# A state space layer's decay matrices from absolute values, without a mask product, with its first scan begun later and two parts of its output split ahead

## The chip, the cores and the metric

The kernel runs as one program on one core of a Trainium2 chip. Five engines of that core work beside each other, each on its own queue of instructions: TensorE (PE, matrix products; its weight loads are listed as PEld), VectorE (DVE), ScalarE (ACT), GpSimd (POOL) and SyncE (SP, which issues most DMAs). The metric is the time of one execution in microseconds on the device. Three runs of the kernel before took 2714.09, 2718.22 and 2720.84; the median is 2718.22.

## The reference, cut to what matters

The program is a chain of eight layers over 512 tokens of width 1024, all in fp32. The layer in question is the second, a Mamba-2 mixer: a projection in, a convolution of four taps with a Silu, 8 groups of 4 heads of width 64 with a state of 128, a scan over 4 chunks of 128 tokens, a gated norm and a projection out.

```python
def step(state, inp):                       # one chunk of 128 tokens
    xc, dtc, bc, cc = inp
    acs = jnp.cumsum(dtc * a, axis=1)
    seg = acs[:, :, None] - acs[:, None, :]
    decay = jnp.exp(jnp.where(mask, seg, -jnp.inf))       # mask: lower triangle
    cb = jnp.einsum("blgn,bsgn->blsg", cc, bc)
    xdt = xc * dtc[..., None]
    y_diag = jnp.einsum("blsg,blsgr,bsgrp->blgrp", cb, decay, xdt)
    y_off = jnp.einsum("blgn,bgrpn->blgrp", cc, state) * jnp.exp(acs)[..., None]
    decay_to_end = jnp.exp(acs[:, -1:] - acs)
    new_state = (state * jnp.exp(acs[:, -1])[..., None, None]
                 + jnp.einsum("bsgn,bsgr,bsgrp->bgrpn", bc, decay_to_end, xdt))
    return new_state, y_diag + y_off
...
y = y + d_skip.astype(jnp.float32).reshape(SSM_GROUPS, SSM_HPG)[:, :, None] * xs
g = (y.reshape(b, s, D_INNER) * jax.nn.silu(z.astype(jnp.float32))).reshape(b, s, SSM_GROUPS, NORM_GROUP)
g = g * lax.rsqrt(jnp.mean(g * g, axis=-1, keepdims=True) + EPS)
g = g.reshape(b, s, D_INNER) * norm_w.astype(jnp.float32)
return g.astype(h.dtype) @ w_out
```

dt is positive and a is negative, so acs falls along a chunk: in the lower triangle seg is never positive, and above it it is never negative.

## The kernel before, in words

**Products.** A product of fp32 operands is made of three matmuls in fp32r (`mm3`, L179 to L181): high part by high part, and the two mixed ones. Weights come by DMA in pieces of 1 MB (`raw`); ACT casts a piece to its high part (wh, L166) and DVE subtracts (wl, L167), for 128x1024 at a time. Activations are split in the same way (xh and xl, ghi and glo, yh and yl, ow). PSUM is used through two pools of four banks each, `psum` (tag ps) and `pacc`; a tile of `psum` is free again when its last reader is done.

**Order.** PE's order in the stage is the order of the code (`manual_schedule(engines={PE})`). The order on the other engines is worked out by a scheduler when the kernel is built, from its own costs for the whole program, so an edit in one stage can shift instructions of ACT and DVE in another.

**The state space stage** runs from about 379 to 853 us. `ssm_groups` goes through 8 groups. For a group, `group` makes four products of 8 steps (`product`, ps_in: B, C and two halves of x, each followed by `conv_silu`) and four z chunks (ps_z, 8 short products each; group 0's z comes with dt ahead of it). It yields 12 times, after each half of a product and each z chunk, and 8 times for group 0. At each yield the scan of the group before is moved one step on (`next(scan, None)`), so a scan's small matmuls lie between products of the next group, which cover its waits.

**A scan** (`ssm_scan`): the first one begins with `ssm_decay`, which makes from dta (dt times a) the sums of a chunk: acsT (the sums on partitions, in two parts), nacs (minus the sums), eacs, etot and edte (exponentials of the sums, of the whole, and of the rest times dt; `dtg` is dt in the scan's order). Then come two pairs of heads: L498 spreads a head's sums over 128 partitions (ps_R, a selecting matrix by acsT), L499 adds a constant `late` in bf16, a large negative number above the diagonal, and ACT takes Exp with the bias nacs for each of the 4 chunks (L503): the decay matrix G. The steps after: transposes of x (ps_x, L511; copies xs L512 on ACT), of B (ps_b, L516), and C by B (ps_cb, L521); on POOL xde = xs by edte (L523) and, after xdt, xs by d_skip (L529); on DVE xdt (L525) and, four times, G by ps_cb (L527). Two steps later, for each chunk, G by xdt into ps_y (L541), the state's products (L543, L546), the sum y, z's gate and a square sum. Last the norm's scale on DVE, the transposes ps_g (L575, two tiles of `psum`) and the copies gt by the norm's weight (L577, ACT).

**The output projection** (`row_steps`) is a generator as well: a step `next(out)` is two products of a 128 wide column with one of the 16 gts, split to high and low by `part`. The last scan has no group left beside it; the steps of `out` lie between its steps, 16 up to its end, and they use parts 0 to 7, which take over the tiles (`xw`) of the layer's input. Parts 8 to 15 follow.

**Other stages that the prediction speaks of.** In the hybrid stage (the seventh, about 2220 to 2440 us) POOL gates pieces of its output weights (L1151), ACT and DVE split them (ow, L172 and L173), and the last of its attention units run meanwhile: scores, Exp to pr (L1310), transposes and copies pT (L1318, by ACT for odd heads), values, and yc, which PE transposes (L1141) before the output products ps_out. In the routed stage (the last) DVE reduces a count to `most` and casts it to an integer, most_i (L1639), which the engines read into a register.

Of the kernel before, what the change touches and what calls it, by code (L numbers as in the profile page):

```python
# [7 lines left out]
F32 = mybir.dt.float32  # L8
# [5 lines left out]
AF = mybir.ActivationFunctionType  # L14
# [4 lines left out]
P = 128  # L19
S = 512  # L20
NT = S // P
# [8 lines left out]
SG, SN, SH = 8, 128, 32  # L30
# [3 lines left out]
def blk(i, n=P):  # L34
    return slice(i * n, (i + 1) * n)
# [42 lines left out]
class Stream:  # L78
# [38 lines left out]
    def next(self, width, eng=None, pieces=1):  # L117
        raw = self.load(width)
        wh = self.pool.tile([P, max(width, 1024)], F32R, tag="wh", name="wh")
        wl = self.pool.tile([P, max(width, 1024)], F32R, tag="wl", name="wl")  # L120
        for i in range(pieces):
            c = blk(i, width // pieces)
            self.K.split(wh[:, c], wl[:, c], raw[:, c], eng)
        return wh, wl


class Kern:
# [220 lines left out]
    def ssm(self, x, wcols, st, V, R):  # L348

        nc, C = self.nc, self.consts  # L350
        with ExitStack() as ctx:
            ctx.enter_context(self.tc.manual_schedule(engines={PE}))
            gtp = self.pool(ctx, "sgt", 16)
            gts, hs = [], []
            out = self.row_steps(16, hs, st, lambda d, p: nc.vector.tensor_add(x[d], x[d], p))

            def part(pool, b, hi, lo):
                hh = pool.tile([P, S], F32R, tag=hi, name="ghi")
                hl = pool.tile([P, S], F32R, tag=lo, name="glo")
                self.split(hh, hl, gts[b])  # L360
                hs.append((hh, hl))

            with ExitStack() as c2:
                scan = self.ssm_groups(c2, gtp, gts, x, wcols, st, V, R)
                xpart = lambda b: part(self.xw, b, f"xh{b}", f"xl{b}")
                next(scan)
                xpart(0)
                xpart(1)
                for i, _ in enumerate(scan):
                    if i < 6:  # L370
                        xpart(i + 2)
                    for _ in range(1 + (i > 5)):
                        next(out)
            hp = self.pool(ctx, "shp", 8)
            for b in range(8, 16):
                part(hp, b, "hh", "hl")
            for _ in out:
                pass

    def ssm_groups(self, ctx, gtp, gts, x, wcols, st, V, R):  # L380

        nc, C = self.nc, self.consts
        t1 = self.pool(ctx, "st1", 1)
        t2 = self.pool(ctx, "st2", 2)
# [7 lines left out]
        E = dict(xw=xw, V=V, R=R)  # L392
# [42 lines left out]

        scan = iter(())
        for g in range(SG):
            for _ in group(g):
                next(scan, None)
            for _ in scan:  # L440
                pass
            scan = self.ssm_scan(g, t1, t2, gtp, gts, E if g == 0 else dict(E))
        for _ in scan:
            yield

# [38 lines left out]
        nc.scalar.activation(E["edte"], perm(pz[:, :W]), AF.Exp)  # L484
        nc.vector.tensor_mul(E["edte"], E["edte"], E["dtg"])

    def ssm_scan(self, g, t1, t2, gtp, gts, E):

        nc, C, V, R = self.nc, self.consts, E["V"], E["R"]
        if g == 0:  # L490
            self.ssm_decay(t1, E)
        bT, cT, xT, zs = E["bT"], E["cT"], (E["xT0"], E["xT1"]), E["zs"]
        bc = lambda t: t[:, g].rearrange("p c h -> p (c h)").unsqueeze(2).to_broadcast([P, 16, 64])
        G = []
        for h in range(4):
            hd = 4 * g + h
            pR = self.psum("ps_R")
            nc.tensor.matmul(pR, C["sel"][:2 * SH, hd:hd + 1].to_broadcast([2 * SH, P]), E["acsT"], start=True, stop=False)  # L498
            nc.tensor.matmul(pR.rearrange("p (a b) -> p a b", b=P), C["identb"],  # L499
                             C["late"].unsqueeze(1).to_broadcast([P, NT, P]), start=False, stop=True)  # L500
            G.append(t1.tile([P, NT, P], F32, tag=f"G{h}", name=f"G{h}"))
            for c in range(NT):
                nc.scalar.activation(G[h][:, c], pR[:, blk(c)], AF.Exp, bias=E["nacs"][:, g, c, h:h + 1])  # L503
            if h % 2:
                yield
        xs = t1.tile([P, 16, 64], F32, tag="xs", name="xs")
# [12 lines left out]
        pc = self.psum("ps_cb")  # L519
# [3 lines left out]
        nc.gpsimd.tensor_mul(xde, xs[:, :12], bc(E["edte"])[:, :12])  # L523
        xdt = t1.tile([P, 16, 64], F32, tag="xdt", name="xdt")
        nc.vector.tensor_mul(xdt, xs, bc(E["dtg"]))  # L525
        for h in range(4):
            nc.vector.tensor_mul(G[h], G[h], pc.rearrange("p (a b) -> p a b", b=P))  # L527
        dsk = R["d_skip"][:, blk(g, 4)].unsqueeze(1).to_broadcast([P, NT, 4])
        nc.gpsimd.tensor_mul(xs.rearrange("p (c h) k -> p c h k", c=NT), xs.rearrange("p (c h) k -> p c h k", c=NT),  # L529
                             dsk.unsqueeze(3).to_broadcast([P, NT, 4, 64]))  # L530
# [7 lines left out]
        for c in range(NT):  # L538
# [5 lines left out]
            if c < NT - 1:  # L544
                pst = self.psum("ps_st")
                nc.tensor.matmul(pst[:, :256], bt[:, c], xde[:, 4 * c:4 * c + 4].rearrange("p a b -> p (a b)"),  # L546
                                 start=True, stop=True)
# [1592 lines left out]
```

## Time and profile before

| | |
|---|---|
| median of three runs | 2718.22 us |
| the profiled execution | 2712.77 us |
| its span | 2710.9 us |
| PE busy | 2601.5 us, 96% |
| DVE busy | 1546.7 us, 57% |
| ACT busy | 1073.6 us, 40% |
| POOL busy | 240.7 us, 9% |

PE is the engine that sets the time; DVE and ACT have room over the span as a whole. A share of the whole span says little of one stage, though, so the rows below are of short stretches. A row of the timeline gives the start and the length in us, the engine, the line and the operation, its tiles (out<-in), the shape, a count, and in brackets the idle time of that engine just before and the instruction that ended it. Matmuls overlap by a part of their length: a product of 512 columns is listed at 0.39 us and the next one begins 0.23 later at the full clock of 2.4 GHz; at 1.2 GHz it is 0.63 and 0.43. A row of the windows gives for each engine its busy time and count in the stretch, PEld between PE and DVE, then the granted clock of PE as a share of full speed, and what the DMAs did.

### The profile page before, as it was taken

To read this page: it belongs to the slowest core of one execution; us is meant where nothing else is said; L and a number is where in the kernel's file an instruction comes from. 1 tells how busy PE (TensorE), PEld (TensorE's weight loads), DVE (VectorE), ACT (ScalarE), POOL (GpSimd) and SP (SyncE) were. 2 spreads that over 40 slices of the span, in tenths; PEclk is the share of its full clock that TensorE was granted. 3 is DMA by queue.
4 is the path that set the end of the run, shared out by engine and by line. 5 is a ranking of instruction groups with operands and counts; after the bars stand their busy time and mean duration, and the time that the engine had idled before them with its cause. 6 is when DMAs were issued, how large, how long until landed. Compare 5 with 4: busy or idle time off the path is not lost. (4 is left out here: it accounts for less than half of the span.)

```text
span 2710.9 us, 32248 instructions
## 1 busy us (share of the span) xinstructions
PE 2601.5 (96%) x12798; PEld 2142.6 (79%) x12798; DVE 1546.7 (57%) x2548; ACT 1073.6 (40%) x1805; POOL 240.7 (9%) x180
## 2 busy tenths in 40 slices
PE   8999999999999999999999999999999989997993
PEld 6888887888878888888888897888888877766782
DVE  5334357676765454656534368655434365567986
ACT  4222245546443222233212245643213234444882
POOL 0000001111100000000000003100000001223324
PEclk9999998999999999999999999999999999898996
DMA  4222221212143243534423221012223222034893
GB/s 153 98 99 99 93 96 47 78 63 78 63 164 132 93 156 118 179 108 160 160 86 109 93 86 61 17 49 94 96 90 109 93 74 88 14 124 168 305 332 114
DMA packets 56472, 300.77 MB, mean 111 GB/s; under 512 B 12002, under 2 KB 12514, under 8 KB 27130
## 3 DMA queue, kind: packets, MB, share of 16 engines
q1 hardware_dynamic: 50096, 285.41, 29.9%
q0 software_dynamic: 4176, 7.39, 0.7%
q10 hardware_dynamic: 2042, 5.84, 0.6%
q8 instruction: 102, 1.67, 0.3%
q14 instruction: 56, 0.46, 0.1%
HBM read 290.68 MB, written 15.75 MB: 113 GB/s over the span
## 5 line engine op out<-in xcount | busy, mean ns | idle before, releaser
L166 ACT CAST wh<-raw 128x1024 fp32r<-128x1024 f32 (+3 forms) x494 | 485.7, 994 | 1100.9 <-PE ps_p L180 378.6
L167 DVE TENSOR_TENSOR wl<-raw,wh 128x1024 fp32r<-128x1024 f32 (+3 forms) x494 | 576.0, 1176 | 385.6 <-ACT wh L166 375.9
L179 PE MATMUL ps_p<-xh,wh 128*128 128x512 f32 x1408 | 550.1, 391 | 6.7 <-ACT xh L172 6.7
L180 PE MATMUL ps_p<-xl,wh 128*128 128x512 f32 x1408 | 549.7, 390 | 0.0
L181 PE MATMUL ps_p<-xh,wl 128*128 128x512 f32 x1408 | 549.5, 390 | 0.0
L179 PEld LDWEIGHTS ps_p<-xh,wh 128*128 128x128 f32 x1408 | 265.4, 188 | 62.4 <-ACT xh L172 6.7
L180 PEld LDWEIGHTS ps_p<-xl,wh 128*128 128x128 f32 x1408 | 265.3, 188 | 56.1 <-DVE xl L173 1.0
L181 PEld LDWEIGHTS ps_p<-xh,wl 128*128 128x128 f32 x1408 | 265.2, 188 | 55.5
L179 PE MATMUL ps_d<-hh,wh 128*128 128x512 f32 x704 | 279.1, 396 | 0.0
L181 PE MATMUL ps_d<-hh,wl 128*128 128x512 f32 x704 | 279.1, 396 | 0.0
L180 PE MATMUL ps_d<-hl,wh 128*128 128x512 f32 x704 | 279.1, 396 | 0.0
L294 DVE TENSOR_TENSOR h<-ps_p,g 128x512 f32<-128x512 f32 x88 | 60.8, 691 | 229.4 <-PE ps_p L181 229.0
L291 DVE TENSOR_TENSOR g<-ps_p,rb 128x512 f32<-128x512 f32 x88 | 60.3, 689 | 177.5 <-PE ps_p L181 177.5
L181 PEld LDWEIGHTS ps_d<-hh,wl 128*128 128x128 f32 x704 | 132.6, 188 | 32.3
L180 PEld LDWEIGHTS ps_d<-hl,wh 128*128 128x128 f32 x704 | 132.6, 188 | 32.3
L179 PEld LDWEIGHTS ps_d<-hh,wh 128*128 128x128 f32 x704 | 132.6, 188 | 32.2
L179 PE MATMUL ps_in<-xh,wh 128*128 128x512 f32 x336 | 140.9, 419 | 0.7 <-ACT wh L166 0.7
L181 PE MATMUL ps_in<-xh,wl 128*128 128x512 f32 x336 | 132.5, 394 | 0.5 <-DVE wl L167 0.5
L180 PE MATMUL ps_in<-xl,wh 128*128 128x512 f32 x336 | 132.1, 393 | 0.0
L181 PEld LDWEIGHTS ps_in<-xh,wl 128*128 128x128 f32 x336 | 63.6, 189 | 15.1 <-DVE wl L167 1.0
L674 POOL TENSOR_TENSOR kro<-prj,kg 128x64 f32<-128x64 f32 x1 | 0.4, 367 | 844.5 <-ACT prj L732 844.5
L961 DVE SCALAR_TENSOR_TENSOR macc<-mraw,c_act,macc 128x1024 f32<-128x1024 f32 x42 | 53.9, 1284 | 37.0 <-DMA mraw<-w_mod 36.7
(577 smaller groups left out, 4224.1 us busy)
## 6 DMA issues: line engine op xcount, KB each, us to landing
raw<-w_ffn SPq DMA_DIRECT2D x131, 1024.0 KB, 4.9
raw<-w_moe SPq DMA_DIRECT2D x48, 1024.0 KB, 7.5
raw<-w_ssm SPq DMA_DIRECT2D x31, 1024.0 KB, 5.1
mraw<-w_mod SPq DMA_DIRECT2D x48, 512.0 KB, 4.4
raw<-w_hyb SPq DMA_DIRECT2D x9, 1024.0 KB, 4.7
expert_out<-zero SPq DMA_DIRECT2D x8, 512.0 KB, 9.9
raw<-w_mla SPq DMA_DIRECT2D x4, 1024.0 KB
yback<-expert_out SPq DMA_DIRECT2D x8, 512.0 KB, 4.6
```

The lines of the kernel that those rows point to most:

```text
L166: a = self.nc.scalar.copy(hi, src)
L167: b = (eng or self.nc.vector).tensor_sub(lo, src, hi.bitcast(F32))
L179: mm(out, ah, bh, start=start, stop=False)
L180: mm(out, ah, bl, start=False, stop=False)
L181: mm(out, al, bh, start=False, stop=stop)
L291: nc.vector.tensor_mul(g, pg, r)
L294: nc.vector.tensor_mul(h, pu, g)
L674: nc.gpsimd.tensor_mul(w, x2, b)
L961: nc.vector.scalar_tensor_tensor(acc, w, ca[:, k:k + 1], acc, op0=ALU.mult, op1=ALU.add)
```

## The change

- `late` and `identb` are no longer multiplied in. ACT takes for each head and chunk the absolute value of the sum's difference (Abs with the bias nacs), and one Exp of 128x512 with scale -1 follows for the head. In the lower triangle that is the same decay; above it it is a value between 0 and 1 in place of 0.
- The mask is put on C by B: `cb` is ps_cb times the triangle, one DVE operation of 128x512 for a group, and G is multiplied by cb, from SBUF, instead of by ps_cb.
- The first scan has a step more, after `ssm_decay`, and in group 1 the steps are given by (0, 0, 1, 2, 2, 1): it begins two steps later, and two later yields take two steps.
- Parts 0 and 1 have tiles of their own (`sgp`), so they are split as soon as their gts are there; `first` is called when scan 5 has been created. In the last scan a step of `out` follows each step from the first on, and two from the ninth on, so that it is 16 at its end as before. The first pair of heads, then an output step, then the second pair now follow ps_g; before, both pairs came first.

```diff
--- before.py
+++ after.py
@@ -361,15 +361,12 @@
                 hs.append((hh, hl))
 
             with ExitStack() as c2:
-                scan = self.ssm_groups(c2, gtp, gts, x, wcols, st, V, R)
-                xpart = lambda b: part(self.xw, b, f"xh{b}", f"xl{b}")
-                next(scan)
-                xpart(0)
-                xpart(1)
+                sp = self.pool(ctx, "sgp", 2, side="right")
+                scan = self.ssm_groups(c2, gtp, gts, x, wcols, st, V, R, lambda: [part(sp, b, "fh", "fl") for b in range(2)])
                 for i, _ in enumerate(scan):
                     if i < 6:
-                        xpart(i + 2)
-                    for _ in range(1 + (i > 5)):
+                        part(self.xw, i + 2, f"xh{i}", f"xl{i}")
+                    for _ in range(1 + (i > 7)):
                         next(out)
             hp = self.pool(ctx, "shp", 8)
             for b in range(8, 16):
@@ -377,7 +374,7 @@
             for _ in out:
                 pass
 
-    def ssm_groups(self, ctx, gtp, gts, x, wcols, st, V, R):
+    def ssm_groups(self, ctx, gtp, gts, x, wcols, st, V, R, first):
 
         nc, C = self.nc, self.consts
         t1 = self.pool(ctx, "st1", 1)
@@ -435,11 +432,14 @@
 
         scan = iter(())
         for g in range(SG):
-            for _ in group(g):
-                next(scan, None)
+            for i, _ in enumerate(group(g)):
+                for _ in range((0, 0, 1, 2, 2, 1)[i] if g == 1 and i < 6 else 1):
+                    next(scan, None)
             for _ in scan:
                 pass
-            scan = self.ssm_scan(g, t1, t2, gtp, gts, E if g == 0 else dict(E))
+            scan = self.ssm_scan(g, t1, t2, gtp, gts, dict(E), None if g else E)
+            if g == 5:
+                first()
         for _ in scan:
             yield
 
@@ -484,23 +484,24 @@
         nc.scalar.activation(E["edte"], perm(pz[:, :W]), AF.Exp)
         nc.vector.tensor_mul(E["edte"], E["edte"], E["dtg"])
 
-    def ssm_scan(self, g, t1, t2, gtp, gts, E):
+    def ssm_scan(self, g, t1, t2, gtp, gts, E, live=None):
 
         nc, C, V, R = self.nc, self.consts, E["V"], E["R"]
-        if g == 0:
-            self.ssm_decay(t1, E)
+        if live is not None:
+            self.ssm_decay(t1, live)
+            E = dict(live, **E)
+            yield
         bT, cT, xT, zs = E["bT"], E["cT"], (E["xT0"], E["xT1"]), E["zs"]
         bc = lambda t: t[:, g].rearrange("p c h -> p (c h)").unsqueeze(2).to_broadcast([P, 16, 64])
         G = []
         for h in range(4):
             hd = 4 * g + h
             pR = self.psum("ps_R")
-            nc.tensor.matmul(pR, C["sel"][:2 * SH, hd:hd + 1].to_broadcast([2 * SH, P]), E["acsT"], start=True, stop=False)
-            nc.tensor.matmul(pR.rearrange("p (a b) -> p a b", b=P), C["identb"],
-                             C["late"].unsqueeze(1).to_broadcast([P, NT, P]), start=False, stop=True)
+            nc.tensor.matmul(pR, C["sel"][:2 * SH, hd:hd + 1].to_broadcast([2 * SH, P]), E["acsT"], start=True, stop=True)
             G.append(t1.tile([P, NT, P], F32, tag=f"G{h}", name=f"G{h}"))
             for c in range(NT):
-                nc.scalar.activation(G[h][:, c], pR[:, blk(c)], AF.Exp, bias=E["nacs"][:, g, c, h:h + 1])
+                nc.scalar.activation(G[h][:, c], pR[:, blk(c)], AF.Abs, bias=E["nacs"][:, g, c, h:h + 1])
+            nc.scalar.activation(G[h], G[h], AF.Exp, scale=-1.0)
             if h % 2:
                 yield
         xs = t1.tile([P, 16, 64], F32, tag="xs", name="xs")
@@ -523,8 +524,10 @@
         nc.gpsimd.tensor_mul(xde, xs[:, :12], bc(E["edte"])[:, :12])
         xdt = t1.tile([P, 16, 64], F32, tag="xdt", name="xdt")
         nc.vector.tensor_mul(xdt, xs, bc(E["dtg"]))
+        cb = t1.tile([P, NT, P], F32, tag="cb", name="cb")
+        nc.vector.tensor_mul(cb, pc.rearrange("p (a b) -> p a b", b=P), C["tri"].unsqueeze(1).to_broadcast([P, NT, P]))
         for h in range(4):
-            nc.vector.tensor_mul(G[h], G[h], pc.rearrange("p (a b) -> p a b", b=P))
+            nc.vector.tensor_mul(G[h], G[h], cb)
         dsk = R["d_skip"][:, blk(g, 4)].unsqueeze(1).to_broadcast([P, NT, 4])
         nc.gpsimd.tensor_mul(xs.rearrange("p (c h) k -> p c h k", c=NT), xs.rearrange("p (c h) k -> p c h k", c=NT),
                              dsk.unsqueeze(3).to_broadcast([P, NT, 4, 64]))
```

Line numbers in the changed kernel are three larger from L500 on or so: L498 became L500, L527 became L530.

**ACT at the first scan.** acsT is the copy of the sums, wh a weight cast, G the decay of one head, bT and cT rows of B and C in their convolution. Before:

```order
L473 CAST acsT<-pr 32x512
L482 ACT_TABLE_LOAD
L482 ACTIVATE eacs<-pa 128x128
L484 ACTIVATE edte<-pz 128x128
L483 ACTIVATE etot<-pt 128x128
L503 ACTIVATE G_2914<-ps_R,nacs 128x128 x4
L503 ACTIVATE G_2922<-ps_R,nacs 128x128 x4
L166 CAST wh<-raw 128x1024
```

Now:

```order
L473 CAST acsT<-pr 32x512
L484 ACT_TABLE_LOAD
L484 ACTIVATE edte<-pz 128x128
L594 ACT_TABLE_LOAD
L594 ACTIVATE bT<-bT 128x512
L483 ACT_TABLE_LOAD
L483 ACTIVATE etot<-pt 128x128
L482 ACTIVATE eacs<-pa 128x128
L166 CAST wh<-raw 128x1024
L503 ACTIVATE G_2965<-ps_R,nacs 128x128 x4
L503 ACTIVATE G_2973<-ps_R,nacs 128x128 x4
L503 ACTIVATE G_2981<-ps_R,nacs 128x128 x4
```

eacs was the first of the three exponentials and is now the last, with two table loads, a Silu of bT and another load ahead of it; and the Abs of four heads stand in a row, ahead of the first Exp of 128x512.

**DVE in scan 1, from xdt to the convolution of cT.** u is the evacuation of a product, wl a weight's low part. Before:

```order
L525 TENSOR_TENSOR xdt<-xs,dtg 128x1024
L584 TENSOR_TENSOR u<-ps_in,rb 128x512
L167 TENSOR_TENSOR wl<-raw,wh 128x1024
L527 TENSOR_TENSOR G_3340<-G_3340,ps_cb 128x512
L527 TENSOR_TENSOR G_3348<-G_3348,ps_cb 128x512
L527 TENSOR_TENSOR G_3368<-G_3368,ps_cb 128x512
L527 TENSOR_TENSOR G_3376<-G_3376,ps_cb 128x512
L590 SCALAR_TENSOR_TENSOR cT<-u,cols,cT 128x511
```

Now (squares is the name that the triangle's tile shows):

```order
L526 TENSOR_TENSOR xdt<-xs,dtg 128x1024
L587 TENSOR_TENSOR u<-ps_in,rb 128x512
L167 TENSOR_TENSOR wl<-raw,wh 128x1024
L528 TENSOR_TENSOR cb<-ps_cb,squares 128x512
L593 SCALAR_TENSOR_TENSOR cT<-u,cols,cT 128x511
L530 TENSOR_TENSOR G_3344<-G_3344,cb 128x512
L530 TENSOR_TENSOR G_3352<-G_3352,cb 128x512
L530 TENSOR_TENSOR G_3372<-G_3372,cb 128x512
L530 TENSOR_TENSOR G_3380<-G_3380,cb 128x512
```

cb is new, and one piece of cT's convolution now stands ahead of the four G; these read cb where they read ps_cb.

**ACT at the end of the hybrid stage's attention.** pr is a head's Exp, pT the copy of its transposes, ow a split output weight, csq the square sum of yc. Before:

```order
L1310 ACTIVATE pr,csm<-ps_s,cmx 128x512
L1318 COPY pT<-ps_pT 128x512
L1310 ACTIVATE pr,csm<-ps_s,cmx 128x512
L1133 ACTIVATE csq,css<-yc 128x256
L1310 ACTIVATE pr,csm<-ps_s,cmx 128x512
L172 ACTIVATE ow<-raw,cols 128x512 x2
L166 CAST yh_17808<-ps_yT 128x128
L1318 COPY pT<-ps_pT 128x512
L172 ACTIVATE ow<-raw,cols 128x512 x2
```

Now:

```order
L1313 ACTIVATE pr,csm<-ps_s,cmx 128x512 x2
L172 ACTIVATE ow<-raw,cols 128x512 x2
L1136 ACTIVATE csq,css<-yc 128x256
L172 ACTIVATE ow<-raw,cols 128x512 x2
L1313 ACTIVATE pr,csm<-ps_s,cmx 128x512
L1321 COPY pT<-ps_pT 128x512
L172 ACTIVATE ow<-raw,cols 128x512 x4
L166 CAST yh_17828<-ps_yT 128x128
L166 CAST yh_17830<-ps_yT 128x128
L1321 COPY pT<-ps_pT 128x512
```

Before, the last copy pT stood behind two casts ow; now it stands behind eight, in three places.

## Rows read from the trace of the kernel before

**Rows 1.** Windows of 20 us: length, five engines' busy us, PE's granted clock.

```profile
420.00:440.00 20.00, 14.68 (x45) 9.82 (x46) 8.78 (x19) 9.88 (x25) 0.00 (x0) 0.66 0.03 3
...
580.00:600.00 20.00, 20.00 (x116) 17.52 (x115) 18.02 (x28) 9.05 (x16) 4.41 (x4) 1.00 0.14 54
...
740.00:760.00 20.00, 17.44 (x108) 14.34 (x107) 11.03 (x28) 16.25 (x39) 0.82 (x2) 0.91 0.17 54
```

**Rows 2.** Two products around a pair of heads, timeline of PE in scan 1.

```profile
477.33 0.39 PE L181 MATMUL ps_in<-xh,wl 128*128 128x512 f32 x1
477.65 0.49 PE L498 MATMUL ps_R<-acsT,sel_r 64*128 64x512 f32 x1
478.07 0.39 PE L499 MATMUL ps_R<-late_r,identb_r 128*128 128x512 bf16 x1
...
479.28 0.39 PE L180 MATMUL ps_in<-xl,wh 128*128 128x512 f32 x1
```

**Rows 3.** Timeline of PE where the first scan begins.

```profile
424.65 1.88 PE L469 MATMUL pr<-squares,dta 128*32 128x128 f32 x8 [5.16 <-DVE dtg L462]
...
428.79 0.79 PE L498 MATMUL ps_R<-acsT,sel_r 64*128 64x512 f32 x1 [0.67 <-ACT eacs L482]
...
436.24 0.50 PE L498 MATMUL ps_R<-acsT,sel_r 64*128 64x512 f32 x1
```

**Rows 4.** Timeline of ACT at the same place, a table load.

```profile
427.17 1.28 ACT L482 ACT_TABLE_LOAD   x1
428.46 0.28 ACT L482 ACTIVATE eacs<-pa 128x128 f32<-128x128 f32 x1
```

**Rows 5.** Timeline of ACT in a later scan.

```profile
569.81 2.18 ACT L503 ACTIVATE G<-ps_R,nacs 128x128 f32<-128x128 f32 x8
...
578.05 1.07 ACT L512 COPY xs<-ps_x 128x512 f32<-128x512 f32 x2 [1.12 <-PE ps_x L511]
...
580.44 0.63 ACT L591 ACTIVATE bT<-bT 128x512 f32<-128x512 f32 x1
```

**Rows 6.** Timelines of DVE, POOL and PE in that scan.

```profile
579.16 1.23 DVE L525 TENSOR_TENSOR xdt<-xs,dtg 128x1024 f32<-128x1024 f32 x1 [0.90 <-ACT xs L512]
...
582.04 2.74 DVE L167 TENSOR_TENSOR wl<-raw,wh 128x1024 fp32r<-128x1024 f32 x1 [0.16 <-ACT wh L166]
584.70 2.47 DVE L527 TENSOR_TENSOR G<-G,ps_cb 128x512 f32<-128x512 f32 x4
...
579.20 2.52 POOL L523 TENSOR_TENSOR xde<-xs,edte 128x768 f32<-128x768 f32 x1 [20.72 <-ACT xs L512]
581.80 1.90 POOL L529 TENSOR_TENSOR xs<-xs,rows 128x1024 f32<-128x1024 f32 x1
...
587.69 1.00 PE L541 MATMUL ps_y<-xdt,G 128*128 128x64 f32 x8
```

**Rows 7.** Timelines of ACT and PE where the last scan begins.

```profile
748.32 2.17 ACT L166 CAST ghi<-gt 128x512 fp32r<-128x512 f32 x4
...
752.06 1.26 ACT L577 ACTIVATE gt<-ps_g,cols 128x512 f32<-128x512 f32 x2
...
752.80 0.50 PE L498 MATMUL ps_R<-acsT,sel_r 64*128 64x512 f32 x1 [2.56 <-ACT gt L577]
```

**Rows 8.** Timelines of DVE, POOL and PE at the hybrid stage's end.

```profile
2389.15 0.74 DVE L173 SCALAR_TENSOR_TENSOR ow<-raw,cols,ow 128x512 fp32r<-128x512 f32 x1
...
2397.47 2.92 DVE L173 SCALAR_TENSOR_TENSOR ow<-raw,cols,ow 128x512 fp32r<-128x512 f32 x1
...
2392.86 9.72 POOL L1151 TENSOR_TENSOR raw<-raw,gate_m 128x1024 f32<-128x1024 f32 x4 [65.68 <-DMA raw<-w_hyb]
...
2404.64 0.66 PE L1141 MATMUL ps_yT<-squares,yc 128*128 128x128 f32 x2 [6.26 <-DVE yc L1136]
```

**Rows 9.** Timelines of DVE and PE at the routed stage's count.

```profile
2491.47 1.23 DVE L167 TENSOR_TENSOR wl<-raw,wh 128x1024 fp32r<-128x1024 f32 x1
...
2492.09 0.47 PE L179 MATMUL ps_gu<-wh,eh 128*128 128x512 f32 x1 [0.98 <-DVE most_i L1639]
```

## The prediction

> **What bounds the kernel now.** I read the windows first, then PE's timeline where a window was not full, then the timelines of ACT, DVE and POOL beside one scan. The reader is to see that the state space stage runs on TensorE: of the 21 windows of 20 us from 440 to 860 all but one are like that of 580 to 600, with PE at 20.00 and clock 1.00. Two of the stretch are not: 420 to 440, where the first scan begins, and 740 to 760, where the last one begins [rows 1]. So a piece of work that leaves PE's queue counts in full, as long as what PE needs next is ready; a piece added on ACT or DVE counts only where PE comes to wait for it. A difference of 0.3% (8.15 us) is about what a measurement of this kernel can tell from none.
>
> **Mask products removed.** Between two products that stand beside a pair of heads lie 479.28 - 477.33 = 1.95 us with two rows of L498 and two of L499 [rows 2]. Without L499 I bound that gap by products at their 0.23 us pitch and by the 0.43 that a start after L498 takes (477.65 to 478.07): 1.01 to 1.41 us. So a pair gives back 0.54 to 0.94; I take 0.8, nearer the upper end, since two weight loads go as well. A scan has two pairs: 1.6 us. Eight scans: 12.8 us gross (8.6 to 15.0).
>
> **Term 1, the first scan.** Before, PE waits 5.16 us for dta (the releaser shown is the copy queued behind it) and 0.67 for eacs, and it works at 1.2 GHz until 436.24, where L498 is back at 0.50 from 0.79 [rows 3]. From 424.65 to 436.24 that is 11.6 us at half speed, some 5.5 lost. Together 11.3. Now eight products more (24 matmuls x 0.228 = 5.47 us) stand ahead of the decay, so PE arrives at 419.49 + 5.47 = 424.96. DVE however has three more pieces queued ahead of dta, an evacuation and two of a convolution, about 2.4 us: dta comes near 427.0 and PE waits 2.1. On ACT the order of the exponentials is turned: a load, edte, a load, a Silu, a load, etot, and eacs last. The first head's L500 reuses the PSUM tile that eacs reads. By the rows, a load takes 1.28 and the next ACTIVATE starts 1.29 after it [rows 4], so eacs ends near 433.7, PE is there at 431.5, and waits 2.2. Behind it I count 0.5 at the first chunk, and 2.3 ahead of the first scan's transposes ps_g: they follow its last chunk after 16 z products (5.75 us), and the chain through y takes about 6.5 plus a weight split that stands between its steps on DVE. Sum of waits 7.1; for the clock, which fell in the rows after waits of 5.16 and 2.56 [rows 1, 3, 7], I add 2: 9.1 after against 11.3 before, and 1.6 for its two pairs: gain 3.8. Bounds: -1 (two falls of the clock as long as the one before) to +9 (all waits covered).
>
> The Trainium skill ("ScalarE: Activation LUTs", section "What ACT_TABLE_LOAD costs") puts a switch at about 2.66 us, 1283 ns and a drain of about 1380. By it two more loads in that chain would take another 2.8 and the term would be 1.0. The trace does not agree: nothing like a drain lies between 427.17 and 428.46 [rows 4].
>
> **Term 2, scans 1 to 6.** ACT has per scan 16 Abs in place of 16 Exp, each 2.18 / 8 = 0.27 [rows 5], and four Exp of 128x512 more; a Silu of that size takes 0.63 [rows 5], so +2.5 us. ACT has room, but one chain gets longer: Abs and Exp of heads 2 and 3, then the two copies of xs, then xdt, the weight split wl, and G. Laid out from 569.5 with those durations, the copies of xs end at 579.95 where they ended at 579.12. On DVE xdt (1.23) then ends near 581.2, u near 581.9, wl near 583.1, the new cb (a quarter of 2.47 = 0.62) near 583.7, one piece of cT's convolution that now stands ahead of G near 584.6, and four G near 587.1 [rows 6]. PE would reach the first chunk at 587.69 - 1.6 = 586.1; before, its fourth head was used near 588.3. So of 1.6 saved per scan 1.15 stay, if POOL doesn't interfere. It can: xde and the product with d_skip run beside this chain, and wl, 1.23 elsewhere, took 2.74 while POOL had the second [rows 6]. G before read PSUM and one SBUF tile; now it reads two SBUF tiles. If DVE's five such pieces and POOL's two go strictly one after another from 579.95 (1.23 + 1.33 + 1.23 + 1.8 + 0.75 + 2.47, 1.33 being what is left of xde's 2.52 behind xdt), G ends at 588.8 and the scan loses 0.5. Between 1.15 and -0.5 I take 0.6, since in the rows POOL's two were over before G began. For scan 1 I take none: ahead of its first Abs stand two casts of the early parts, 1.1 us. So 5 x 0.6 = 3.0 (-2.5 to 8).
>
> **Term 3, the last scan.** Before, the third L498 waits 2.56 for a PSUM tile that gt frees, the clock falls, to a mean of 0.91 over that window [rows 1], so another 0.09 x 20 = 1.8 lost [rows 7]. Together 4.4. Now a step of two output products (6 x 0.23 = 1.4) stands between the pairs, and two of four casts ahead of gt (0.54 each) are gone, as the early parts are split right behind the first scan's gt: gt comes about 1 us earlier. That leaves waits of 1.0 and 0.35 there. The gain is 3.0, if the clock stays up and if G is ready for chunk 0, whose chain on ACT is longer here too, by four Exp of 0.63; I take 2.0 (-0.5 to 3). After chunk 2 fewer products stand in cover now, which I cost at nothing, since the z product's place is taken by the ones moved forward and y's chain has two more steps to run.
>
> **Term 4, the hybrid stage.** The scheduler has also shuffled ACT and DVE there. PE waits 6.26 for yc before its output products, while POOL gates raw for 9.72 us in four tiles; DVE's ow then took 2.92 instead of 0.74 [rows 8]. In the new order ACT's casts of ow, which wait for POOL's last tile near 2402.6, stand ahead of a copy of pT that PE's last attention product needs. Output products begin near 2408 instead of 2405: -3 (+1 to -6).
>
> **Term 5, the routed stage.** A wl of 1.23 now stands on DVE ahead of most_i, for which PE waits 0.98 already [rows 9]: -1 (0 to -1.2).
>
> What else moves (two loads more at the first scan, one weight transfer of SP ahead of the register load, DVE's order in the first feed-forward) has no reader waiting in the rows; cost zero, and a microsecond each if one does.
>
> **Sum.** 3.8 + 3.0 + 2.0 - 3 - 1 = 4.8 us faster. The profiled execution took 2712.77 with a span of 2710.9; it would take 2708.0. The median of the runs lies 5.4 higher, 2718.22, so the forecast is 2713.4 there.
>
> **Rivals.**
> R1, full gain. G is ready before PE asks, ACT and DVE slip into gaps, and the hybrid stage's new order costs nothing because POOL's tiles set its time in either order. For it: with PE full in 20 of 21 windows, ACT's and DVE's small delays have found cover so far. Against: the chain in rows 5 and 6 had no slack of 1.6. Time: 5.8 (term 1 without the clock) + 6 x 1.6 + 3.0 = 18.4 less: 2700.
>
> R2, it doesn't do what it says. The products go, and PE waits for G exactly as much longer, as G's chain and not PE's queue sets the first chunk. For it: G ended within a microsecond of its use. Against: part of the chain starts from PE's own L500, which come earlier. Time: term 2 is nil, 1.8 less: 2716.4.
>
> R3, slower. DVE's G and POOL's products keep each other waiting, as wl and ow did [rows 6, 8]. G ends at 588.8, 2.7 after PE arrives; a wait of 2.56 made the clock fall and cost 1.8 more [rows 1, 7]. Each of scans 1 to 6 then loses 0.5 + 1.8 = 2.3: 13.8, less 5.8 of terms 1 and 3, plus 4 of terms 4 and 5: 12.0 slower, 2730. It decides once G ends past about 588.5, 1.4 us later than laid out. Against: in the rows POOL was done at 583.7, ahead of G.
> The Trainium skill ("SBUF — State Buffer", section "SBUF: two separate sides") says that a DVE operation with two SBUF inputs and a GpSimd operation that reads SBUF lock each other out for a whole instruction. By that rule the chain is at its serial end, 588.8. The trace agrees in kind: 2.74 against 1.23.
>
> **How the numbers follow.** Forecast 0.45, with its own range 2707 to 2719 (three quarters of it within 0.3%, from 2710.1 up); R1 0.28; R2 0.13; R3 0.14. Faster: 0.28 + 0.11 = 0.39. Within: 0.34 + 0.13 = 0.47. Slower: 0.14. The range runs from 2696 to 2724: below it lies a fifth of R1 (0.06), above it R3 (0.14).
>
> **What would show it.** Term 1: PE's idle before pr down to 2 from 5.2, idle before the first L500 up to about 2. Term 2: in a scan like the one at 565, a gap without L499 near 1.15, and an idle of about 1 before the first chunk, released by G. Term 3: idle 2.56 gone from the last scan. Term 4: output products of the hybrid stage later against their stage's start. R1 has full windows through all scans, R3 windows with a clock under 1 in each scan. I am wrong if scans 1 to 6 shift by something other than products and G, or if the hybrid stage moves by more than 6.

## The result

The changed kernel takes 2740.83 us in the median of four runs (2738.18 to 2744.48), the kernel before 2716.3 beside it: a ratio of 1.0097, with a 95% interval of 1.0082 to 1.0111. It is slower by 24.5 us, where 4.8 us faster was forecast. Its profiled execution took 2744.48 with a span of 2742.2, 31.3 more than before. That is more than the 24.5 of the medians, as the one profile is of the slowest of its four runs and the other of a run 3.5 under the median.

Where the 31.3 lie is read from four marks on PE's timeline, the first ps_zdt of the state space stage, the first ps_p behind it, and in the hybrid stage the first ps_v and the first ps_out (each number is rounded by itself):

| stretch | before | after | more |
|---|---|---|---|
| ahead of the state space stage | 379.7 | 381.1 | 1.4 |
| state space stage, ps_zdt to ps_p | 473.9 | 492.7 | 18.8 |
| ps_p to ps_v | 1391.7 | 1392.1 | 0.4 |
| hybrid stage, ps_v to ps_out | 159.6 | 169.2 | 9.5 |
| ps_out to the end | 306.0 | 307.1 | 1.1 |

Windows of the changed kernel, the columns as in [rows 1]:

```profile
580.00:600.00 20.00, 18.41 (x85) 14.53 (x84) 16.04 (x19) 13.78 (x25) 3.50 (x2) 0.93 0.15 53
...
740.00:760.00 20.00, 19.82 (x120) 17.88 (x121) 16.77 (x33) 6.98 (x17) 2.21 (x3) 0.91 0.15 54
```

The scans, which were full, are full no longer: PE idles 1.59 us in the first of these windows and the clock dips. One scan shows why. Timeline of PE around a pair of heads and at the first chunk:

```profile
576.59 0.39 PE L181 MATMUL ps_in<-xh,wl 128*128 128x512 f32 x1
576.91 0.72 PE L500 MATMUL ps_R<-acsT,sel_r 64*128 64x512 f32 x2
577.55 0.50 PE L179 MATMUL ps_in<-xh,wh 128*128 128x512 f32 x1
577.89 0.40 PE L180 MATMUL ps_in<-xl,wh 128*128 128x512 f32 x1
...
584.05 1.03 PE L512 MATMUL ps_x<-squares,xT 128*128 128x128 f32 x8
...
595.67 0.94 PE L544 MATMUL ps_y<-xdt,G 128*128 128x64 f32 x4 [1.15 <-DVE G L530]
596.79 0.43 PE L544 MATMUL ps_y<-xdt,G 128*128 128x64 f32 x2 [0.17 <-DVE G L530]
597.39 0.69 PE L544 MATMUL ps_y<-xdt,G 128*128 128x64 f32 x2 [0.17 <-DVE G L530]
...
599.26 0.63 PE L180 MATMUL ps_in<-xl,wh 128*128 128x512 f32 x1
```

The pair is cheaper: 577.89 - 576.59 = 1.30 us where it was 1.95 [rows 2]. But the first chunk waits for G, takes a head each 0.6 us as G comes, and products behind it run at 0.63 us, the clock being down. The chain that ends with G, timelines of ACT, DVE and POOL in the same scan:

```profile
586.67 1.11 ACT L513 COPY xs<-ps_x 128x512 f32<-128x512 f32 x2
...
585.81 2.32 DVE L593 SCALAR_TENSOR_TENSOR bT<-u,cols,bT 128x511 f32<-128x511 f32 x3 [1.54 <-ACT bT L590]
588.05 2.50 DVE L526 TENSOR_TENSOR xdt<-xs,dtg 128x1024 f32<-128x1024 f32 x1
...
591.07 2.60 DVE L167 TENSOR_TENSOR wl<-raw,wh 128x1024 fp32r<-128x1024 f32 x1
593.59 0.68 DVE L528 TENSOR_TENSOR cb<-ps_cb,squares 128x512 f32<-128x512 f32 x1
594.19 0.74 DVE L593 SCALAR_TENSOR_TENSOR cT<-u,cols,cT 128x511 f32<-128x511 f32 x1
594.85 2.49 DVE L530 TENSOR_TENSOR G<-G,cb 128x512 f32<-128x512 f32 x4
...
587.86 1.61 POOL L524 TENSOR_TENSOR xde<-xs,edte 128x768 f32<-128x768 f32 x1 [21.54 <-ACT xs L513]
590.69 1.90 POOL L532 TENSOR_TENSOR xs<-xs,rows 128x1024 f32<-128x1024 f32 x1 [1.23 <-DVE xdt L526]
```

Counted from ps_x, which PE issues itself (at 584.05, and at 577.36 before), the copies of xs end 3.73 us on (1.76 before), xdt 6.50 (3.03), wl 9.62 (7.42) and G 13.29 (9.81) [rows 5, 6]. PE is free for the first chunk after 10.47; before, it began the chunk after 10.33. xdt is behind xde now: before it began 0.04 us ahead of it and took 1.23; now DVE was still at bT's convolution when the copies ended, for 0.35 us more; xde was first, 587.86 against 588.05, and xdt took 2.50. wl stood behind the product with d_skip in both kernels. The Trainium skill ("SBUF — State Buffer", section "SBUF: two separate sides") has such pieces of DVE and GpSimd lock each other out for a whole instruction; the rows agree: xde ends at 589.47, and xdt 1.08 later. The expectations below call this the port.

### The profile page after: what moved, and what is told of

It reads as the page before. It is cut to its first block, busy times and chain, and to the rows that moved or that the text cites. A ratio compares the mean times of both kernels' runs of the same rounds, so it can differ in the third digit from the quotient of the medians.

```text
span 2742.2 us, 32226 instructions
## 1 busy us (share of the span) xinstructions
PE 2622.4 (96%) x12763; PEld 2158.4 (79%) x12766; DVE 1564.1 (57%) x2556; ACT 1092.0 (40%) x1839; POOL 229.8 (8%) x180
## 5 line engine op out<-in xcount | busy, mean ns | idle before, releaser
L179 PEld LDWEIGHTS ps_in<-xh,wh 128*128 128x128 f32 x336 | 65.7, 196 | 18.4 <-issue 4.6
L180 PEld LDWEIGHTS ps_in<-xl,wh 128*128 128x128 f32 x336 | 65.6, 195 | 12.9
```

Of the source, the lines that this page charges most:

```text
L179: mm(out, ah, bh, start=start, stop=False)
L180: mm(out, ah, bl, start=False, stop=False)
```

## The experiments

The stage's length and the period are read as above (the period is the mean distance of ps_g over scans 1 to 6); a second number is a second profile. The medians are of 4 to 12 runs, the other columns of one profile each.

| kernel | median us | ratio, interval | stage us | period us | ps_v to ps_out |
|---|---|---|---|---|---|
| before | 2716 | | 473.9 | 45.63 | 159.6 |
| changed (and e13) | 2740.8 | 1.0097 (1.0082 to 1.0111) | 492.7, 496.0 | 47.77, 48.08 | 169.2, 163.4 |
| e1 Abs, Exp, cb alone | 2733.4 | 1.0070 (1.0052 to 1.0088) | 492.3 | 48.35 | 164.4 |
| e2 late start alone | 2722.3 | 1.0021 (1.0010 to 1.0032) | 472.1 | 45.63 | 169.2 |
| e3 early parts alone (e16) | 2706.8 | 0.9982 (0.9966 to 0.9998) | 471.0, 471.2 | 45.63, 45.63 | 156.6, 166.8 |
| e4 cb alone | 2717.3 | 1.0007 (0.9994 to 1.0020) | 476.6 | 45.88 | 166.8 |
| e5 no mask product (e14) | 2712.7 | 0.9981 (0.9968 to 0.9994) | 461.7, 461.7 | 44.39, 44.39 | 169.2, 169.2 |
| e6 e1, xde from xdt | 2730.2 | 1.0050 (1.0031 to 1.0068) | 488.9 | 47.82 | 159.7 |
| e7 e6, d_skip on ACT | 2710.3 | 0.9982 (0.9968 to 0.9996) | 466.8 | 44.65 | 161.5 |
| e8 e1, short Exp | 2713.2 | 0.9992 (0.9978 to 1.0006) | 472.8 | 45.60 | 159.7 |
| e9 changed, old order | 2738.2 | 1.0067 (1.0046 to 1.0087) | 496.0 | 48.68 | 166.8 |
| e10 changed, e7's edits | 2703.0 | 0.9951 (0.9939 to 0.9963) | 462.6 | 44.65 | 159.6 |
| e11 e7 and early parts | 2708.1 | 0.9966 (0.9954 to 0.9978) | 467.5 | 44.63 | 158.4 |
| e12 e11, mask kept (e15) | 2714.1 | 0.9986 (0.9973 to 0.9999) | 471.1, 468.0 | 45.63, 45.63 | 166.7, 161.3 |

A stage's length holds the clock of the first scan too, which is not the same in every execution. Between the two profiles of e12, one kernel, the first ps_g comes 94.1 and 91.0 us into the stage (94.2 before), 3.1 apart. Windows 430 to 440 of both, e12 and then e15:

```profile
430.00:440.00 10.00, 10.00 (x30) 6.79 (x30) 2.85 (x4) 6.10 (x18) 0.00 (x0) 0.70 0.07 8
```

```profile
430.00:440.00 10.00, 10.00 (x45) 7.41 (x46) 4.84 (x6) 7.78 (x21) 0.00 (x0) 1.00 0.30 107
```

So a difference of 3 us between two stages can be this alone; the period is free of it.

**e1, e2, e3: the change taken apart.** Each is the kernel before with one of its parts, in the lines of the change.

e1:

```diff
-            nc.tensor.matmul(pR.rearrange("p (a b) -> p a b", b=P), C["identb"],
-                             C["late"].unsqueeze(1).to_broadcast([P, NT, P]), start=False, stop=True)
...
+                nc.scalar.activation(G[h][:, c], pR[:, blk(c)], AF.Abs, bias=E["nacs"][:, g, c, h:h + 1])
+            nc.scalar.activation(G[h], G[h], AF.Exp, scale=-1.0)
...
+        nc.vector.tensor_mul(cb, pc.rearrange("p (a b) -> p a b", b=P), C["tri"].unsqueeze(1).to_broadcast([P, NT, P]))
+            nc.vector.tensor_mul(G[h], G[h], cb)
```

> The kernel before with the decay by Abs and Exp, no mask product and cb on DVE, and nothing else of the change. Theory P (the chain to G got longer: xs copied later on ACT, xdt behind POOL's xde on the shared port, cb and a piece of cT on DVE): scans 1 to 7 wait for G as in the changed kernel, where they lost 1.2 to 4.6 us each and 18 in all; so 2728 to 2736, with the hybrid stage as before. Theory L (the late start and its shifted steps are what costs, the decay by Abs alone gives its 1.3 us per scan): 2706 to 2712.

e2:

```diff
+                for _ in range((0, 0, 1, 2, 2, 1)[i] if g == 1 and i < 6 else 1):
...
+        if live is not None:
+            self.ssm_decay(t1, live)
+            E = dict(live, **E)
+            yield
```

> The kernel before with the first scan begun two steps later and nothing else. Theory P: the scans 1 to 7 keep their 45.65 us period; the order of ACT and DVE in the hybrid stage is that of the changed kernel, so 9 us are lost there and 1.3 in the routed stage, less 0 to 4 for scan 0: 2722 to 2727. Theory L: the scans lose here, 2730 or more, with periods over 46.5 us. If the hybrid stage's 9 us come from somewhere else than the order: 2712 to 2717.

e3:

```diff
+            if g == 5:
+                first()
...
-                    for _ in range(1 + (i > 5)):
+                    for _ in range(1 + (i > 7)):
```

> The kernel before with parts 0 and 1 split ahead and the output steps spread as in the change, nothing else. All theories: the last scan's wait of 2.56 us for gt shrinks to about 1 and the clock holds; 2712 to 2716, periods of scans unchanged at 45.65.

The decay by Abs alone costs 18.4 us in the stage, as theory P has it, and the median with it (1.0070). The late start leaves the period alone, so theory L falls. Its stage is 1.9 shorter, where term 1 without its pairs had 2.2, but no gain is shown by that: e2's first ps_g comes 5.2 sooner than before, but only 2.0 sooner than in the second profile of e12. Then 2.0 are lost in scan 1, where the clock falls behind a wait of 1.82 ahead of ps_g, and 1.4 in the last scan. Its median is 6.1 higher, of which the order in the hybrid stage explains 2.4 (below).

The early parts gain 2.9 and 2.7 in the stage in two profiles. It lies in the last scan, 2.8 shorter in both (32.7 from ps_g to ps_g, 35.5 before), where the wait of 2.56 for gt is gone and the clock holds. e3's median, 2706.8, is below the range expected: seven of its ten runs took 2703 to 2708 and three 2716 to 2718. Its two profiles, one of either kind, have 156.6 and 166.8 us in the hybrid stage.

**e4: cb alone.**

```diff
+        nc.vector.tensor_mul(cb, pc.rearrange("p (a b) -> p a b", b=P), C["tri"].unsqueeze(1).to_broadcast([P, NT, P]))
         for h in range(4):
-            nc.vector.tensor_mul(G[h], G[h], pc.rearrange("p (a b) -> p a b", b=P))
+            nc.vector.tensor_mul(G[h], G[h], cb)
```

> The kernel before, mask product kept, with cb made by DVE in SBUF and G multiplied by it: cb's part of the change alone. Theory P: G is 1.3 us later in each scan (cb 0.62 and a piece of cT 0.66), which is 0.3 to 0.8 more than the slack at the fourth head: 0.2 to 0.8 us per scan, 2718 to 2723. Theory S (two SBUF inputs of G against POOL are the price): 2 us or more per scan, 2730 or more.

The period grows by 0.25 us, as theory P has it; the median, 2717.3, is just under its range. In scans 0 to 6 G from two SBUF tiles took 2.48 there and 2.49 in the changed kernel, against 2.47 from PSUM: POOL is done by then. Theory S falls for these, and cb is the small part of their price. The last scan is another matter: there G runs beside POOL. Timelines of DVE and POOL before, then of DVE, POOL and PE in e4:

```profile
761.02 2.47 DVE L527 TENSOR_TENSOR G<-G,ps_cb 128x512 f32<-128x512 f32 x4
...
759.92 2.51 POOL L523 TENSOR_TENSOR xde<-xs,edte 128x768 f32<-128x768 f32 x1 [18.92 <-ACT xs L512]
```

```profile
760.64 4.75 DVE L529 TENSOR_TENSOR G<-G,cb 128x512 f32<-128x512 f32 x4
...
761.41 2.22 POOL L531 TENSOR_TENSOR xs<-xs,rows 128x1024 f32<-128x1024 f32 x1
...
764.24 0.43 PE L543 MATMUL ps_y<-xdt,G 128*128 128x64 f32 x2 [1.65 <-DVE G L529]
```

By ps_cb, G took its 2.47 beside POOL's work; by cb it took 4.75, PE waited and the clock fell (0.83 from 760 to 770), and the last scan is 4.2 us longer (39.7 from ps_g to ps_g, 35.5 before). That is theory S, in one scan of eight. The stage shows 2.7 of it alone, as the first ps_g came 3.0 sooner.

**e5: the product's own worth.**

```diff
-                nc.scalar.activation(G[h][:, c], pR[:, blk(c)], AF.Exp, bias=E["nacs"][:, g, c, h:h + 1])
+                nc.scalar.activation(G[h][:, c], pR[:, blk(c)], AF.Exp, bias=E["edte"][:, g, c, h:h + 1])
```

and L499's product left out.

> The kernel before with the mask product of each head left out and Exp with another bias (edte, so that it stays bounded): 16 Exp a scan as before, G by ps_cb as before; the mask and the bias are left out of the decay. Theory P: nothing delays G here, so each pair gives its 0.65 us, 1.3 a scan, 10 in all: 2704 to 2709. Rival W (G's chain sets the first chunk whatever PE does, and the saving turns into waits): 2713 to 2717, with an idle of 1 us ahead of each first chunk.

The period falls by 1.24 and the stage by 12.2, 3 or so of it by the clock of the first scan: the saving is there when nothing holds G up. Windows of this kernel, full at full clock:

```profile
580.00:600.00 20.00, 20.00 (x136) 18.53 (x135) 17.19 (x37) 8.35 (x18) 2.65 (x3) 1.00 0.15 53
```

Its median fell by 2.5 only, outside the range expected, because of the hybrid stage (169.2, below). Rival W falls.

**e6, e7, e8: which part of the chain.** All start from e1. e6 makes xde from xdt, e7 also takes the product with d_skip to ACT and writes the Exp of heads 2 and 3 behind the copies of xs (ACT's order stays):

```diff
-        nc.vector.tensor_mul(E["edte"], E["edte"], E["dtg"])
...
-        nc.gpsimd.tensor_mul(xde, xs[:, :12], bc(E["edte"])[:, :12])
         nc.vector.tensor_mul(xdt, xs, bc(E["dtg"]))
+        nc.gpsimd.tensor_mul(xde, xdt[:, :12], bc(E["edte"])[:, :12])
...
-        nc.gpsimd.tensor_mul(xs.rearrange("p (c h) k -> p c h k", c=NT), xs.rearrange("p (c h) k -> p c h k", c=NT),
-                             dsk.unsqueeze(3).to_broadcast([P, NT, 4, 64]))
+        for h in range(4):
+            v = xs.rearrange("p (c h) k -> p c h k", c=NT)[:, :, h]
+            nc.scalar.activation(v, v, AF.Copy, scale=R["d_skip"][:, 4 * g + h:4 * g + h + 1])
```

> Kernel e1 (Abs, Exp and cb alone, 2733) with xde made from xdt and not from xs, so that POOL can't begin ahead of DVE's xdt. Theory P, port: xdt takes 1.23 instead of 2.50 and G ends 1.2 us earlier in each scan if wl then comes ahead of the product with d_skip, 2720 to 2726; if wl stands behind xde and d_skip's product instead, nothing is gained, 2730 to 2734. Theory A (ACT's later copies of xs alone are the price): no gain, 2731 to 2735, though xdt is shorter.

> Kernel e6 with the product with d_skip on ACT too (four ACTIVATE of 128x256) and the Exp of heads 2 and 3 written after the copies of xs (the scheduler leaves them ahead). POOL then has xde alone beside the chain. Theory P, port: wl ends about 1.7 us earlier than in e1 and G 2.3 us, the wait ahead of the first chunk goes: 2712 to 2718. Theory A: ACT has another 1.2 us per scan, 2733 to 2740.

e8:

```diff
-            nc.scalar.activation(G[h], G[h], AF.Exp, scale=-1.0)
+            nc.scalar.activation(G[h][:, 0, :1], G[h][:, 0, :1], AF.Exp, scale=-1.0)
```

> Kernel e1 with each Exp of 128x512 cut to 128x1 (the exponential of the rest is left out), so ACT's extra work per scan is about 0.8 instead of 2.5 us, and cb, the port and the order of POOL stay. Theory A: the copies of xs come about 0.8 us earlier, and with xdt ahead of the third piece of bT's convolution xdt starts before xde: 2712 to 2720. Theory P with the port alone: xdt still 2.50 long, 2728 or more.

Timelines of DVE, POOL and PE, first of e6, then of e7; ps_x began at 577.35 and 570.73:

```profile
581.36 1.22 DVE L521 TENSOR_TENSOR xdt<-xs,dtg 128x1024 f32<-128x1024 f32 x1
...
583.10 2.21 DVE L167 TENSOR_TENSOR wl<-raw,wh 128x1024 fp32r<-128x1024 f32 x1
...
587.53 2.48 DVE L527 TENSOR_TENSOR G<-G,cb 128x512 f32<-128x512 f32 x4
...
584.19 2.88 POOL L529 TENSOR_TENSOR xs<-xs,rows 128x1024 f32<-128x1024 f32 x1
...
588.36 0.94 PE L541 MATMUL ps_y<-xdt,G 128*128 128x64 f32 x4 [0.53 <-DVE G L527]
```

```profile
574.75 1.22 DVE L524 TENSOR_TENSOR xdt<-xs,dtg 128x1024 f32<-128x1024 f32 x1
...
576.48 2.21 DVE L167 TENSOR_TENSOR wl<-raw,wh 128x1024 fp32r<-128x1024 f32 x1
...
579.32 2.50 DVE L530 TENSOR_TENSOR G<-G,cb 128x512 f32<-128x512 f32 x4
...
581.06 1.25 PE L545 MATMUL ps_y<-xdt,G 128*128 128x64 f32 x8
```

e6 shortens xdt to 1.22, but the product with d_skip then falls between DVE's last pieces, and G ends 12.66 us after ps_x, 0.63 sooner only. wl did come ahead of that product, and still the median is 2730.2 where theory P had 2720 to 2726; its interval overlaps e1's, so e6 by itself speaks for neither theory. e7 leaves xde alone on POOL, G ends at 11.09, and the wait is gone though ACT carries 1.7 us more: the period is 44.65, near e5's, and the stage is 25.4 us shorter than e1's (the median, 2710.3, is a little under the range). Theory A falls as the sole cause. But e8, with ACT's share cut and xdt still 2.50 long, is back at 45.60, and its median, 2713.2, is where theory A had it and not at the 2728 or more of the port alone: G ends 12.03 after ps_x there. So no single link is the cause. ACT's later copies (2.0), xdt behind xde (1.3) and cb with the piece of cT (1.3) lengthen a chain that ended 0.5 ahead of the chunk, by 3.5 in all, as wl stands closer behind xdt now; taking away most of ACT's extra work or most of POOL's brings most of the loss back.

**e9, e13 to e16: the hybrid stage.** e9 is the changed kernel with two transposes of the last scan done twice, which turned the scheduler's order in the hybrid stage back, row for row.

```diff
+            for c in range(2 if g == 7 else 0):
+                nc.tensor.transpose(pg[:, blk(c)], y[:, c, blk(j)], C["ident"])
```

> The changed kernel with two of the last scan's eight transposes ps_g done twice (0.2 us), which turns the scheduler's order of the hybrid and the routed stage back to that of the kernel before. Theory H (the other order is what costs there): the stretch from ps_v to ps_out takes 157 to 167 us as in the four kernels with the old order, not 169.2, and most_i stands ahead of wl again; 2729 to 2734 where the changed kernel took 2740.8. Rival (the stage drifts by itself): 2738 to 2743.

> The changed kernel once more, for a second profile. Theory H (its order of ACT and DVE costs in the hybrid stage): from ps_v to ps_out 169 us again. Theory C (only the clock decides there: it stays at 1.2 GHz through the stretch in some executions, whatever the order): 157 to 170, by execution.

> Kernel e5 once more (mask and bias left out of the decay); it has the changed kernel's order in the hybrid stage. Theory H: 169 us again from ps_v to ps_out. Theory C: its runs went from 2703 to 2714, so an execution near 2704 has 159 to 161 there, at 2.4 GHz from some point of the stretch on.

> Kernel e12 once more; it has the old order, and took 166.7 us from ps_v to ps_out. Theory H: the old order allows both, nothing is told. Theory C: an execution near 2705 has 157 to 160 there, one near 2716 has 166 to 167 again.

> Kernel e3 once more; old order, 156.6 us in its profile. Theory C: an execution near 2717 (three of its ten runs) has 166 to 167 there, one near 2705 has 157.

With the old order the stretch took 166.8 in e9's profile, and e9 ran from 2727 to 2743.5; theory H falls as the cause of the 9.5. Windows from 5 us behind the first ps_yT to ps_out, one row of each kernel in this order: before, changed, changed again (e13), e12, e12 again (e15), each in its own fence:

```profile
2374.90:2404.90 30.00, 23.24 (x142) 17.01 (x142) 25.78 (x55) 18.06 (x44) 9.72 (x4) 0.90 0.21 70
```

```profile
2392.10:2435.10 43.00, 39.89 (x142) 28.61 (x142) 27.21 (x53) 20.37 (x46) 9.32 (x4) 0.50 0.14 49
```

```profile
2394.00:2431.30 37.30, 28.52 (x143) 21.63 (x142) 25.15 (x54) 20.41 (x46) 10.15 (x4) 0.73 0.16 57
```

```profile
2367.40:2408.00 40.60, 39.73 (x142) 28.70 (x142) 22.78 (x55) 18.23 (x44) 9.32 (x4) 0.50 0.15 52
```

```profile
2370.90:2400.90 30.00, 23.23 (x142) 16.96 (x142) 25.86 (x55) 18.04 (x44) 9.72 (x4) 0.90 0.20 70
```

The same 142 matmuls take 23 us or 40 of PE, by the granted clock: 0.50 throughout, or back at full speed on the way. That changes between two profiles of one kernel (the changed one, e12 with e15, e3 with e16), so it belongs to an execution. The order matters less: at 0.50 throughout, 169.2 us with the new order (the changed kernel, e2, e5 and e14) and 166.7 to 166.8 with the old (e4, e9, e12, e16), so 2.4. Why the clock comes back in one execution and not in another stays open.

**e10, e11, e12: the repaired change.** e10 is the changed kernel with e7's edits to xde and d_skip and one transpose done twice for the old order; e11 is e7 with the early parts, and so without the late start; e12 keeps the mask product and has the other edits of e11.

```diff
-        nc.vector.tensor_mul(E["edte"], E["edte"], E["dtg"])
...
+        nc.gpsimd.tensor_mul(xde, xdt[:, :12], bc(E["edte"])[:, :12])
...
+            nc.scalar.activation(v, v, AF.Copy, scale=R["d_skip"][:, 4 * g + h:4 * g + h + 1])
...
+            for c in range(1 if g == 7 else 0):
+                nc.tensor.transpose(pg[:, blk(c)], y[:, c, blk(j)], C["ident"])
```

> The changed kernel with xde made from xdt, the product with d_skip on ACT, and one transpose done twice, which gives the old order of the hybrid stage. Theory P: period of scans 44.65 as in e7; the state space stage 462 us (473.9 before, less 7.1 as e7, 1.9 as e2, 2.9 as e3): 2702 to 2708, faster than both kernels. Theory A (ACT carries too much): scans as in the changed kernel, 2725 or more.

> Kernel e7 (Abs, Exp and cb, xde from xdt, d_skip on ACT) with the early parts of e3, the first scan begun as before. Theory P: e7's gain and e3's add, 7.1 and 2.9 us in the stage: 2704 to 2709. If the gt wait of the last scan, 3.39 in e7, is not shortened by the early parts: 2709 to 2712.

> The kernel before (mask product and 16 Exp kept) with xde from xdt, d_skip's product on ACT and the early parts. Theory P: PE was full in the scans, so the freed port brings nothing there and only the last scan gains: 2710 to 2715, period 45.65. If POOL's share of the port had cost the kernel before as well: period under 45.4 and 2707 or less.

All three medians came as theory P had them. e10 is faster than both kernels, 0.9951 of the kernel before, its stage at 462.6 us. e12 shows that the freed port is worth nothing by itself in the scans: PE was full at 45.63. e11's stage, though, is 467.5 where the gains of e7 and e3 add up to 463.9. Its wait for gt is down to 0.75, but in the last scan PE then waits 2.21 and 1.38 for G, so the early parts give 1.2 there and not 2.8. e10's last scan is 3.7 shorter than e11's; why was not taken apart, so the late start's worth stays open.

## Why the prediction was wrong

The state space stage lost 18.8 us where terms 1 to 3 had it gain 8.8.

**The mask product** was right in kind: 1.95 to 1.30 us a pair, so 0.65 where 0.8 was taken, inside the bounds of 0.54 to 0.94.

**Term 2 is the step that failed**: "Between 1.15 and -0.5 I take 0.6, since in the rows POOL's two were over before G began." In these scans G was not the piece that POOL held up; xdt and wl were, ahead of it. The layout put G 11.3 us after ps_x by its times, the serial end 13.0, and it came at 13.29, past the end that was taken as the worst; the serial sum leaves out u and cb, 0.68 each, which stand in the same queue. I had seen wl at 2.74 beside POOL [rows 6] and still laid it out at 1.23; and that xdt began 0.04 us before xde I took for an order, while it was a race that 0.35 us of bT's convolution turned. Scans 2 to 6 lost 10.7 us (526.31 to 765.15 for ps_g, against 519.57 to 747.72) where 3.0 were to be gained. Term 2 has nothing for the clock: the distance from ps_g to ps_g is 46.9 where the clock holds and 48.2 to 48.5 where it falls, in three of these five scans, so 6 of the 10.7 come of the waits and the rest of the clock. Rival R3 comes nearest, with POOL and the clock, though it had G as the piece that is blocked and the clock down in each scan. Scan 1, taken as nil, lost 4.6.

**Term 1** forecast a gain of 3.8 to the first scan's end; ps_g of scan 0 came 0.7 later in the stage. The waits were laid out well: 7.9 in all, 7.1 forecast. Timeline of PE in the changed kernel:

```profile
428.36 1.03 PE L469 MATMUL pr<-squares,dta 128*32 128x128 f32 x8 [1.99 <-DVE dtg L462]
...
435.18 0.73 PE L500 MATMUL ps_R<-acsT,sel_r 64*128 64x512 f32 x2 [1.52 <-ACT etot L483]
...
451.43 0.69 PE L544 MATMUL ps_y<-xdt,G 128*128 128x64 f32 x2 [1.63 <-DVE G L530]
...
476.01 1.55 PE L578 MATMUL ps_g<-squares,y 128*128 128x128 f32 x8 [1.82 <-DVE y L572]
```

2.1, 2.2 and 2.3 were forecast for the first, second and fourth. The third row, and 0.94 for xdt ahead of it, is term 2's failure again, at 0.5 in the sum. What was mis-sized is the clock, with 2: its mean was 0.84 from 430 to 440 and 0.66 from 450 to 460, so it stood at 1.2 GHz for about 10 us, some 5 lost (an estimate, half of the time, as term 1 has it for the kernel before). Nor is a gain measured from one profile of the first scan safe, as e12 shows. The table loads were read right, 1.28 each:

```profile
430.02 1.28 ACT L484 ACT_TABLE_LOAD   x1
431.31 0.28 ACT L484 ACTIVATE edte<-pz 128x128 f32<-128x128 f32 x1
431.61 1.28 ACT L594 ACT_TABLE_LOAD   x1
432.90 0.63 ACT L594 ACTIVATE bT<-bT 128x512 f32<-128x512 f32 x1
```

No drain is seen behind either load. The Trainium skill ("ScalarE: Activation LUTs", section "What ACT_TABLE_LOAD costs") gives about 2.66 us for a switch; the rows disagree, at 1.29 from load to next start.

**Term 3** had the early parts right (e3: 2.9) and missed that the last scan's chain is held up the most: chunk 0 waited 1.84 for xdt and 1.86 for G, and the scan lost 2.7 instead of gaining 2.0. It took G as ready there; but here POOL does hold up G, as in e4. Two heads took 2.98 us, and the four of another scan 2.49. Timelines of PE and DVE:

```profile
769.19 1.07 PE L500 MATMUL ps_R<-acsT,sel_r 64*128 64x512 f32 x2 [0.75 <-ACT gt L580]
...
779.94 1.04 PE L544 MATMUL ps_y<-xdt,G 128*128 128x64 f32 x6 [1.84 <-DVE xdt L526]
...
782.84 0.69 PE L544 MATMUL ps_y<-xdt,G 128*128 128x64 f32 x2 [1.86 <-DVE G L530]
...
779.81 2.98 DVE L530 TENSOR_TENSOR G<-G,cb 128x512 f32<-128x512 f32 x2
```

**Term 4** forecast 3 for the other order; 2.4 were measured at one clock. The further 7 of that profile are the clock's, and with them the stage moved by more than the 6 that were named as a sign of being wrong.

**Term 5** was right: PE waits 2.25 for most_i where it waited 0.98 [rows 9], with a wl of 1.23 ahead of it.

```profile
2520.58 1.23 DVE L167 TENSOR_TENSOR wl<-raw,wh 128x1024 fp32r<-128x1024 f32 x1 [0.17 <-ACT wh L166]
2521.72 0.15 DVE L1642 CAST most_i<-most 128x1 int32<-128x1 f32 x1
```

The sign also came from weighing: R1 had 0.28 and R3 0.14, though the rows already showed the block on wl that R3 rests on.

## What to carry to other kernels

Work taken from a full engine pays only while the chain to its next operand has slack; lay that chain out from what the operations took beside their neighbours, not from what they take alone, and compare its end with the arrival. Two operations of DVE and POOL that are released by the same event are a race, and a few tenths elsewhere turned it here; a data dependence (xde from xdt) fixes the order. And judge a stage by its own marks: a whole run can hide a gain of 12 us in one stage behind the clock of another.

## What the runs showed of the hardware

The length of a wait did not say whether the clock fell. In e6 PE idled 0.96 us of the window from 580 to 600 and the clock fell in each of scans 2 to 6, 47.8 us from ps_g to ps_g. In the changed kernel it idled 1.59 in that window; behind the same waits the clock fell in three of these scans (48.2 to 48.5) and held in two (46.9), and in e9 it fell in all five. What decides it was not found. In the hybrid stage TensorE stayed at 1.2 GHz for over 40 us with PE busy 39.9 of 43 us, and left it in other executions of the same kernel. A product by DVE of PSUM and SBUF tiles and one of two SBUF tiles took the same, 2.47 and 2.49 us for four, with POOL idle; with POOL at work the first still took 2.47 and the second 4.75 (the last scan, before and e4).
